# Where the eight S5 gate blocks stand, and VectorE's order, in a one-core backbone step

## The chip, the core and the metric

The kernel runs on one NeuronCore of a Trainium2 chip. The metric is the device time of one execution in microseconds (us). Five engines work side by side, each through its own queue in order: TensorE (PE in the rows, PEld its weight loads), VectorE (DVE), ScalarE (ACT), GpSimd (POOL) and SyncE (SP), which here only issues DMAs.

## The reference, cut to what matters

One step of a two-layer hybrid backbone over 1024 latent and 256 context tokens, in float32. The part around the change is the even layer: one projection of the modulated input, a bidirectional S5 state-space scan, and the gate with which the S5 output is multiplied.

```python
proj = h @ pe['w_in']
u_a, z_a, q, k, v, z_b = jnp.split(proj, [...], axis=-1)
y_a, hf_re, hf_im = _s5_bidir(u_a, ...)          # scan over the tokens, both directions
g_a = jax.nn.gelu(y_a)
y_a = g_a * jax.nn.sigmoid(g_a @ pe['w_glu'] + pe['b_glu'])
y_a = y_a * jax.nn.silu(z_a)                     # z_a: eight blocks of 128 columns, the "gate blocks"
...
o = _diff_attn(q_r, k_all, v_all, lam)           # keys and values: cached context and new ones
```

## The kernel before

All activations are held transposed, 128 channels by 1280 tokens (`NT`; 1024 latent and 256 context). A projection block of 128 columns is `project_steps`: three chunks of 512, 512 and 256 tokens, each eight steps over the 1024 input channels, each step three matmuls (`mm3`, lines 46 to 48: the float32 operands are split into a high and a low part). The function yields after half of each 512 chunk and after each chunk, so a block has five pieces. ScalarE and VectorE make the low part of the weights ahead (`split`, lines 41 and 42): starting block j emits the loads and the splits of block j + 1, and there are two sets of weight buffers.

A gate block is `z_steps`: after each chunk ScalarE takes a tanh out of PSUM (L907) and VectorE multiplies (L908), which frees the PSUM buffer (tag `acc`, four of them); at the end the 128 x 1280 result is written to `dZa` for a later stage.

`stage_a` ends with these parts. First the q and k blocks (`qk_block`), spread over two scans (`ssm.scan`, L527 to L583). A scan is a chain of small operations on VectorE, 31 steps of five (L527, L529, L530, L531, L532), then a correction loop (L579 to L583) in four parts, each written to memory (`dz`, L584). Outside of `manual_schedule` a planner sets each engine's order from costs of its own, not the source.

Then the S5 outputs, for j = 0 to 7, in pools of their own, which take over memory of the scan. `c_weights(j)` makes four groups of weights on VectorE (three operations each, L456 to L458), 24 small matmuls (`kp`, L612 to L614), copies to `kt` on ScalarE (L616), an addition to `kt` on VectorE (L620) and eight DMAs from `kt` to `m` (L623). `load_c(j)` loads `u` and `zc`. `c_out(j)` is 24 matmuls (`y`, L645 to L647), four GELUs on ScalarE (L649) and eight DMAs to `dG` that ScalarE's queue issues (L653). In iteration j, `c_weights(j + 1)` comes first, then gate block j + 1, then `c_out(j)`. Only TensorE is held to the order of the source there; the planner orders VectorE and ScalarE.

After the output of j = 4 stands `cache_parts`: four times, a 512 KB piece of the cached keys (twice) or values (twice) is loaded to a tile `cx`, split by ScalarE (`chi`, L41) and VectorE (`cx`, L42), and both parts are written back to memory, in four DMAs for keys and two for values. Its tiles come from the pool `zx`, which has three buffers and also holds the gate blocks' results. Attention (first matmuls L994) follows.

Of the kernel before, what the change touches and what calls it, by code (L numbers as in the profile page):

```python
# [10 lines left out]
F32 = mybir.dt.float32  # L11
# [10 lines left out]
NT = LS + LP  # L22
# [16 lines left out]
def split(nc, src, hi, lo, le=None):  # L39

    nc.scalar.copy(hi, src)  # L41
    (le or nc.gpsimd).tensor_sub(lo, src, hi.bitcast(F32))  # L42


def mm3(nc, out, whi, wlo, xhi, xlo, start, stop):
    nc.tensor.matmul(out, whi, xhi, start=start, stop=False)  # L46
    nc.tensor.matmul(out, whi, xlo, start=False, stop=False)  # L47
    nc.tensor.matmul(out, wlo, xhi, start=False, stop=stop)  # L48
# [318 lines left out]
class Weights:  # L367
# [5 lines left out]
    def next(s, key, steps=False):  # L373

        if s.gen is None:
            s.start()
        while s.step():
            pass
        w, s.gen = s.ahead, None
        assert s.rest.pop(0)[0] == key  # L380
        if s.rest and s.rest[0][1] is not None:
            s.start()
            while not steps and s.step():
                pass
        return w
# [16 lines left out]
def project(*args, **k):  # L402
    for _ in project_steps(*args, **k):
        pass
# [23 lines left out]
def raw_dma(nc, dst, src):  # L428

    nc.sync.dma_start(dst.bitcast(F32), src.bitcast(F32))  # L430
# [249 lines left out]
def stage_a(c, wp):  # L680

    nc, tc, a, o = c.nc, c.tc, c.a, c.o
    c.wlo = nc.vector
    dt = lambda n, shape, t=F32: [c.dram.tile(shape, t, name=f"{n}{i}") for i in range(HB)]
    c.dU = dt("dU", [128, 8, NCH])
    c.dG = dt("dG", [128, T, NCH])
    c.dQh, c.dQl = dt("dQh", [128, NT], F32R), dt("dQl", [128, NT], F32R)
    c.dK = [dt(f"dK{m}_", [128, NT], F32R) for m in range(2)]
    c.dZa = dt("dZa", [128, NT])
    with ExitStack() as es:  # L690
        pool = lambda n, b, **k: es.enter_context(tc.tile_pool(name=n, bufs=b, **k))
        ev = pool("ev", 2)
        ssm = Ssm(c)
        c.wfp = [c.wf1, pool("wf", 1)]

        def chunk(j, evac, i, w, part=(0, KC)):
            o, n = CH[i]
            if part[0] == 0:
                chunk.p = ps.tile([128, 512], F32, name="acc", tag="acc")
            for k in range(*part):  # L700
                mm3(nc, chunk.p[:, :n], w[0][:, k], w[1][:, k], c.hhi[:, k, o:o + n], c.hlo[:, k, o:o + n], k == 0, k == KC - 1)
            if part[1] == KC:
                evac(chunk.p[:, :n], o, n)

        def new_u(j):
            x = ev.tile([128, T, NCH], F32, name="x", tag="x")
            xv = x.rearrange("q t (k i) -> q t k i", i=NS)

            def evac(p, off, n):
                if off < LS:  # L710
                    nc.scalar.copy(xv[:, off // 128:off // 128 + 4, :, 1:], p.rearrange("q (t i k) -> q t k i", t=4, k=SEG))
                else:
                    nc.scalar.copy(xv[:, :, :, 0], p.rearrange("q (t c) -> q t c", c=CP))

            def done():
                for t in range(T):
                    nc.sync.dma_start(c.dU[j][t * N:(t + 1) * N].rearrange("n g c -> g n c"), x[:, t])
            return evac, done

        def u_block(j):  # L720
            evac, done = new_u(j)
            project(c, ps, c.w.next(('in', j)), c.hhi, c.hlo, evac)
            done()

        def qk_block(h, is_k):
            x = ev.tile([128, NT], F32, name="x", tag="x")
            sc = 1.0 if is_k else 0.125
            project(c, ps, c.w.next(('in', (24 if is_k else 16) + h)), c.hhi, c.hlo,
                    lambda p, off, n: nc.scalar.activation(x[:, off:off + n], p, AF.Copy, scale=sc))
            xs = rp.tile([128, LS], F32, name="xs")  # L730
            for q in range(4):
                nc.scalar.dma_start(xs[q * 32:(q + 1) * 32], x[(q ^ 1) * 32:(q ^ 1) * 32 + 32, 0:LS])
            if is_k:
                nc.scalar.dma_start(o['new_cache_k'][h], x[:, LS:NT])
            nc.vector.tensor_mul(x[:, 0:LS], x[:, 0:LS], rc[:, 0])
            nc.vector.tensor_mul(xs, xs, rc[:, 1])
            nc.vector.tensor_add(x[:, 0:LS], x[:, 0:LS], xs)
            hi = rp.tile([128, NT], F32R, name="xhi")
            lo = x.bitcast(F32R)
            split(nc, x, hi, lo, nc.vector)  # L740
            if is_k:
                for m in range(2):
                    for r, t in enumerate((hi, lo)):
                        raw_dma(nc, c.dK[m][h][r * 64:(r + 1) * 64], t[m * 64:(m + 1) * 64])
            else:
                raw_dma(nc, c.dQh[h], hi)
                raw_dma(nc, c.dQl[h], lo)

        ET = mybir.EngineType
        with tc.tile_pool(name="ps0", bufs=3, space=PSUM) as ps, tc.manual_schedule(engines={ET.PE, ET.DVE, ET.Activation, ET.Pool}):  # L750
            startup(c, ps, new_u, chunk)
        ps = pool("ps", 4, space=PSUM)
        c.sc = pool("ssk", 1, side="right")
        neg_lambda(c)
        ssm_tables(c)
        st = pool("sst", 2)
        ts = [ssm.c_tables(st, j) for j in range(2)]
        with tc.tile_pool(name="rp", bufs=1) as rp, tc.tile_pool(name="zp", bufs=1) as zp, \
                tc.tile_pool(name="ssb", bufs=2) as sb:
            for j in range(2, 4):  # L760
                u_block(j)
            z = ssm.new_z(zp, 0)
            ssm.powers(zp, 0)
            for j in range(4):
                ssm.b_side(sb, ps, j, z)
            rc = rp.tile([128, 2, LS], F32, name="rope")
            nc.sync.dma_start(rc, a['rope'])
            for j in range(4, 8):
                u_block(j)
            qk = [(h, is_k) for is_k in (True, False) for h in range(8)]  # L770

            def scan(h):
                for _ in ssm.scan(zp, h, z):
                    if qk:
                        qk_block(*qk.pop(0))

            for _ in range(KA):
                qk_block(*qk.pop(0))
            scan(0)
            z = ssm.new_z(zp, 1)  # L780
            ssm.powers(zp, 1)
            for j in range(4, 8):
                ssm.b_side(sb, ps, j, z)
            for _ in range(KB):
                qk_block(*qk.pop(0))
            scan(1)
            while qk:
                qk_block(*qk.pop(0))
        with tc.tile_pool(name="ssc", bufs=2) as sb, tc.tile_pool(name="zx", bufs=3) as zx:
            with tc.manual_schedule(engines={ET.PE}):  # L790
                def gate(j):
                    x = zx.tile([128, NT], F32, name="zx", tag="zx")
                    for _ in z_steps(c, ps, x, j):
                        pass
                    nc.sync.dma_start(c.dZa[j], x)

                gate(0)
                w = ssm.c_weights(sb, ps, 0, *ts.pop(0))
                uz = ssm.load_c(sb, 0)
                for j in range(8):  # L800
                    if j < 7:
                        nuz = ssm.load_c(sb, j + 1)
                        if j < 6:
                            ts.append(ssm.c_tables(st, j + 2))
                        nw = ssm.c_weights(sb, ps, j + 1, *ts.pop(0))
                        gate(j + 1)
                    ssm.c_out(sb, ps, j, *w, *uz)
                    w, uz = nw, nuz
                    if j == 4:
                        cache_parts(c, zx)  # L810
        c.wfp = [c.wf1]
    c.wlo = nc.gpsimd


KA, KB = 4, 2


def startup(c, ps, u_block, chunk):
# [82 lines left out]
def z_steps(c, ps, x, j, steps=False, late=None):  # L901

    nc = c.nc

    def evac(p, off, n):
        t = x[:, off:off + n]
        nc.scalar.activation(t, p, AF.Tanh, scale=0.5)  # L907
        nc.vector.scalar_tensor_tensor(t, t, 1.0, p, op0=OP.add, op1=OP.mult)  # L908
    return project_steps(c, ps, c.w.next(('in', 8 + j), steps), c.hhi, c.hlo, evac, late=late)
# [1119 lines left out]
```

## Time and profile before

| what | value |
|---|---|
| median of 3 runs | 2831.46 us (2827.33 to 2838.45) |
| the profiled execution | 2831.44 us, its span 2829.4 us |
| TensorE busy in the span | 2566.0 us (91%) |
| VectorE busy | 1772.5 us (63%) |
| ScalarE busy | 1075.5 us (38%) |
| mean granted TensorE clock | 0.958 of full speed |

All times in the rows are counted from the start of the span. Two stretches matter: the tail of the second scan (510 to 592 us) and the S5 outputs (592 to 807 us). In the rows, a letter q behind an engine's name (SPq, ACTq) marks its queue issuing a DMA, and the brackets hold the idle time before an instruction and what ended it.

### The profile page before, as it was taken

How to read it: one execution, taken by the hardware profiler on the slowest of the kernel's cores; microseconds unless marked ns; L12 is line 12 of the kernel's file. 1: busy time of each engine (PE TensorE's matmuls, PEld its weight loads, DVE VectorE, ACT ScalarE, POOL GpSimd, SP SyncE). 2: the span in 40 equal slices, each digit the busy share in tenths (PEclk: the TensorE clock that was granted, in tenths of full speed). 3: DMA queues.
4: the chain of work that ended last, by engine and by line, in shares of the span. 5: the costliest groups of instructions: out<-in, count | busy, mean ns of one | idle time of the engine just before them, and what ended most of it. 6: DMA issues, size and time to landing. Idle time of an engine off the chain costs nothing.

```text
span 2829.4 us, 40030 instructions
## 1 busy us (share of the span) xinstructions
PE 2566.0 (91%) x14905; PEld 2244.0 (79%) x14905; DVE 1772.5 (63%) x3636; ACT 1075.5 (38%) x2136; POOL 512.7 (18%) x434
## 2 busy tenths in 40 slices
PE   8999889159879999999988989988999999999998
PEld 6788778148768788887876878867999989999786
DVE  6879988984336787777876866675234435654332
ACT  3342243012246666666754221464223333322311
POOL 0000000000012332323331000005223334332321
PEclk9999999579999999999999999999999999999999
DMA  6445663256752222222226883322322136654422
GB/s 229 172 129 132 175 208 117 91 160 192 227 142 76 80 73 66 90 83 79 78 65 161 295 274 123 116 82 84 106 79 75 58 102 226 199 171 151 149 79 93
DMA packets 249130, 374.01 MB, mean 132 GB/s; under 512 B 39492, under 2 KB 172134, under 8 KB 245350
## 3 DMA queue, kind: packets, MB, share of 16 engines
q1 hardware_dynamic: 226376, 324.47, 36.7%
q10 hardware_dynamic: 22416, 46.33, 5.0%
q8 instruction: 117, 1.92, 0.3%
q14 instruction: 77, 0.63, 0.1%
q0 software_dynamic: 144, 0.66, 0.1%
HBM read 254.06 MB, written 104.73 MB: 127 GB/s over the span
## 4 chain that ended last, share of the span: by engine, by line
PE 46%; DVE 10%; ACT 5%; DMA 4%; issue 2%; POOL 2%; SPq 0%; DVEq 0%; ACTq 0%; POOLq 0%
PE pf L46 6%; PE pf L47 6%; PE pf L48 6%; PE oa L48 4%; PE oa L46 4%; PE oa L47 4%; PE acc L46 2%; PE acc L48 2%; PE acc L47 2%; ACT e L1020 2%; DVE mx L1010 2%; DVE atl L1054 2%; DMA owf<-w_out_o 1%; DVE e L1038 1%; PE atp L1050 1%
## 5 line engine op out<-in xcount | busy, mean ns | idle before, releaser
L46 PE MATMUL acc<-hhi,whi 128*128 128x512 f32 (+1 forms) x1152 | 421.2, 366 | 20.1 <-DVE zx L908 7.5
L48 PE MATMUL acc<-hhi,wlo 128*128 128x512 f32 (+1 forms) x1152 | 415.4, 362 | 25.8 <-DVE wlo L42 25.6
L47 PE MATMUL acc<-hlo,whi 128*128 128x512 f32 (+1 forms) x1152 | 417.1, 362 | 0.9 <-DVE hlo L218 0.2
L1041 POOL TENSOR_TENSOR e<-e,e 128x1024 f32<-128x1024 f32 x64 | 152.6, 2384 | 1124.6 <-ACT e L1040 850.9
L48 PEld LDWEIGHTS acc<-hhi,wlo 128*128 128x128 f32 x1152 | 221.6, 192 | 62.5 <-DVE wlo L42 31.3
L46 PEld LDWEIGHTS acc<-hhi,whi 128*128 128x128 f32 x1152 | 221.7, 192 | 58.5 <-ACT O L1063 11.1
L46 PE MATMUL oa<-owh,oyh 128*128 128x512 f32 x640 | 254.6, 398 | 8.2 <-DVE t L1379 5.1
L48 PE MATMUL oa<-owh,oyl 128*128 128x512 f32 x640 | 253.4, 397 | 1.0 <-POOL oyl L42 1.0
L47 PE MATMUL oa<-owl,oyh 128*128 128x512 f32 x640 | 254.1, 397 | 0.0
L47 PEld LDWEIGHTS acc<-hlo,whi 128*128 128x128 f32 x1152 | 221.6, 192 | 34.8 <-DVE hlo L218 4.6
L1020 ACT ACTIVATE e<-X,mx 128x1024 f32<-128x1024 f32 x128 | 142.9, 1116 | 121.2 <-DVE mx L1014 118.4
L41 ACT CAST whi<-wf 128x512 fp32r<-128x512 f32 x146 | 89.3, 620 | 208.7 <-DMA wf<-w_glu 41.8
L1010 DVE TENSOR_REDUCE mx<-X 128x1 f32<-128x1024 f32 x128 | 155.1, 1212 | 9.7 <-PE X L995 9.7
L42 POOL TENSOR_TENSOR wlo<-wf,whi 128x512 fp32r<-128x512 f32 x64 | 82.8, 1294 | 419.6 <-ACT whi L41 403.8
L46 PEld LDWEIGHTS oa<-owh,oyh 128*128 128x128 f32 x640 | 121.4, 190 | 38.6 <-ACT gt L1280 4.0
L42 DVE TENSOR_TENSOR wlo<-fold,whi 128x512 fp32r<-128x512 f32 x94 | 84.7, 914 | 106.5 <-ACT whi L41 105.5
L48 PEld LDWEIGHTS oa<-owh,oyl 128*128 128x128 f32 x640 | 121.4, 190 | 29.7 <-POOL oyl L42 1.4
L47 PEld LDWEIGHTS oa<-owl,oyh 128*128 128x128 f32 x640 | 121.5, 190 | 27.9
L1053 ACT CAST ath<-atp 128x512 fp32r<-128x512 f32 (+1 forms) x208 | 99.4, 514 | 103.1 <-PE atp L1050 101.6
L46 PE MATMUL pf<-heh,whi 128*128 128x322 f32 x400 | 126.1, 319 | 9.9 <-ACT heh L1549 8.3
L1054 DVE TENSOR_TENSOR atl<-atp,ath 128x512 fp32r<-128x512 f32 (+1 forms) x208 | 115.2, 578 | 17.0 <-ACT ath L1053 17.0
L47 PE MATMUL pf<-hel,whi 128*128 128x322 f32 x400 | 125.6, 314 | 0.1
(448 smaller groups left out, 6665.7 us busy)
## 6 DMA issues: line engine op xcount, KB each, us to landing
wf<-w_in_e SPq DMA_DIRECT2D x96, 256.0 KB
raw<-w_fno SPq DMA_DIRECT2D x16, 1024.0 KB
mw<-w_mod SPq DMA_DIRECT2D x24, 512.0 KB
stg<-w_modT SPq DMA_DIRECT2D x24, 512.0 KB
u<-dU SPq DMA_DIRECT2D x16, 640.0 KB
dz<-z SPq DMA_DIRECT2D x8, 1280.0 KB
zc<-dz SPq DMA_DIRECT2D x16, 640.0 KB
qh<-dQh SPq DMA_DIRECT2D x160, 64.0 KB
```

The costliest lines, as they stand in the source:

```text
L41: nc.scalar.copy(hi, src)
L42: (le or nc.gpsimd).tensor_sub(lo, src, hi.bitcast(F32))
L46: nc.tensor.matmul(out, whi, xhi, start=start, stop=False)
L47: nc.tensor.matmul(out, whi, xlo, start=False, stop=False)
L48: nc.tensor.matmul(out, wlo, xhi, start=False, stop=stop)
L1010: v.tensor_reduce(t.mx[:, 0, m:m + 1], t.X[m], axis=AX.X, op=OP.max, negate=True)
L1020: nc.scalar.activation(t.e[m][:, :LS], t.X[m], AF.Exp, bias=b, accum_out=t.sums[:, 0, m:m + 1])
L1038: v.scalar_tensor_tensor(e[0][:, :nk], e[1][:, :nk], t.r, e[0][:, :nk], op0=OP.mult, op1=OP.add)
L1041: nc.gpsimd.tensor_add(e[0][:, nk:], e[0][:, nk:], e[1][:, nk:])
L1050: nc.tensor.transpose(p[:, i], t.e[0][:, (b + i) * 128:(b + i + 1) * 128], c.ident)
L1053: nc.scalar.copy(hi, p[:, :w])
L1054: return lambda: v.tensor_sub(t.al[:, b:b + w, o], p[:, :w], hi.bitcast(F32))
```

## The change

Gate blocks 0 to 3 are now written at the end of the scan's part of the source, outside of `manual_schedule`, with result tiles from pool `ev`. Gate blocks 4 to 7 are one generator. `fill(n)` runs its next n pieces (halves of a 512 chunk, or the 256 chunk): two pieces before the outputs' loop, then two ahead of each `c_out(j)` and one behind it. That makes 2 + 3 per iteration, so the 20 pieces are used up in iteration 5. Within that part VectorE too is now held to the order of the source, `cache_parts` included.

```diff
             while qk:
                 qk_block(*qk.pop(0))
+            for j in range(GE):
+                x = ev.tile([128, NT], F32, name="x", tag="x")
+                for _ in z_steps(c, ps, x, j):
+                    pass
+                nc.sync.dma_start(c.dZa[j], x)
         with tc.tile_pool(name="ssc", bufs=2) as sb, tc.tile_pool(name="zx", bufs=3) as zx:
-            with tc.manual_schedule(engines={ET.PE}):
-                def gate(j):
-                    x = zx.tile([128, NT], F32, name="zx", tag="zx")
-                    for _ in z_steps(c, ps, x, j):
-                        pass
-                    nc.sync.dma_start(c.dZa[j], x)
-
-                gate(0)
+            with tc.manual_schedule(engines={ET.PE, ET.DVE}):
+                def gates():
+                    for j in range(GE, 8):
+                        x = zx.tile([128, NT], F32, name="zx", tag="zx")
+                        yield from z_steps(c, ps, x, j)
+                        nc.sync.dma_start(c.dZa[j], x)
+                rest = gates()
+
+                def fill(n):
+                    for _ in range(n):
+                        next(rest, None)
+                fill(2)
                 w = ssm.c_weights(sb, ps, 0, *ts.pop(0))
                 uz = ssm.load_c(sb, 0)
                 for j in range(8):
...
                         nw = ssm.c_weights(sb, ps, j + 1, *ts.pop(0))
-                        gate(j + 1)
+                    fill(2)
                     ssm.c_out(sb, ps, j, *w, *uz)
+                    fill(1)
                     w, uz = nw, nuz
                     if j == 4:
                         cache_parts(c, zx)
+                fill(100)
...
+GE = 4
```

What this does to the engines' orders, at three places. All other rows of the five queues, from attention on, stand as before.

VectorE in the second scan, one piece of the difference (+ the changed kernel). L531 and L532 end a scan step, L920 is the changed kernel's number for the gate's multiplication, `wlo` the low part of a block's weights.

```order
 L531 TENSOR_TENSOR m_4096<-m_4096,z 128x320
+L920 SCALAR_TENSOR_TENSOR x<-x,acc 128x256
 L532 TENSOR_TENSOR z<-m_4096,m_4097 128x64x5
+L42 TENSOR_TENSOR wlo<-wf,whi 128x512
 L527 TENSOR_TENSOR m_4103<-A8r,z 128x320
 L529 TENSOR_TENSOR m_4104<-A8i,z 64x320
 L530 TENSOR_TENSOR m_4104<-A8i,z 64x320
 L531 TENSOR_TENSOR m_4103<-m_4103,z 128x320
+L42 TENSOR_TENSOR wlo<-wf,whi 128x512
 L532 TENSOR_TENSOR z<-m_4103,m_4104 128x64x5
+L920 SCALAR_TENSOR_TENSOR x<-x,acc 128x512
```

Sixteen such instructions come into the scan: ten multiplications (seven of 512 columns and three of 256: gate blocks 1 to 3 and the first chunk of block 4) and six splits of weights (for blocks 3, 4 and 5).

VectorE around the caches, before: one split of a cached piece stands among the weights of j = 6, three more behind the weights and the `kt` of j = 7.

```order
L457 TENSOR_TENSOR t_6415<-tab,tabc 128x576
L42 TENSOR_TENSOR cx<-cx,chi 128x1024
L458 TENSOR_TENSOR cw_6413<-t_6414,t_6415 128x576
...
L620 TENSOR_TENSOR kt<-kt,dd 16x8x16
L42 TENSOR_TENSOR cx<-cx,chi 128x1024 x3
L908 SCALAR_TENSOR_TENSOR zx<-zx,acc 128x512 x2
```

And after, the same place: all four stand in a row, right behind the multiplication of gate block 7's first chunk and ahead of the weights of j = 6.

```order
L920 SCALAR_TENSOR_TENSOR zx<-zx,acc 128x256
L42 TENSOR_TENSOR wlo<-wf,whi 128x512 x2
L920 SCALAR_TENSOR_TENSOR zx<-zx,acc 128x512
L42 TENSOR_TENSOR cx<-cx,chi 128x1024 x4
L456 TENSOR_TENSOR t_6336<-tab,tabc 128x576
L457 TENSOR_TENSOR t_6337<-tab,tabc 128x576
L458 TENSOR_TENSOR cw_6335<-t_6336,t_6337 128x576
```

SP's queue at that place, after: the loads of `cx` and the writes of its parts follow each other, behind the loads of `u` and `zc` of j = 6, with the DMAs to `m` of j = 6 behind them. Before, DMAs of the outputs (`m`, `zc`, `u`, `dZa`) stood between them.

```order
L445 DMA u<-dU_92 128x1280
L632 DMA zc<-dz_151 128x2x640
L351 DMA wf<-w_in_e 128x512
L665 DMA cx<-cache_k 128x4x256
L430 DMA dKc_6289<-chi 64x1024
L430 DMA dKc_6289<-cx 64x1024
L430 DMA dKc_6290<-chi 64x1024
L430 DMA dKc_6290<-cx 64x1024
L665 DMA cx<-cache_k 128x4x256
```

ScalarE's four `chi` casts likewise stand in a row now, behind the DMA issues to `dG` of j = 4 and the tanh of gate block 7's first chunk.

## Rows read from the trace of the kernel before

**Rows 1.** Waits of TensorE, 510 to 803 us: who waited, total us, times, longest.

```profile
PE kp L612 <- DVE cw L458: 82.3, 3, 81.4
```

**Rows 2.** Busy us of each engine in stretches (count), granted clock, DMA share, GB/s.

```profile
core 0: us, PE busy (x) PEld busy (x) DVE busy (x) ACT busy (x) POOL busy (x), PEclk, DMA share, GB/s
510.00:592.00 82.00, 0.57 (x5) 0.39 (x5) 74.00 (x167) 3.81 (x8) 0.00 (x0) 0.52 0.29 96
592.00:611.00 19.00, 11.89 (x96) 7.76 (x95) 18.48 (x28) 2.19 (x4) 0.00 (x0) 0.68 0.78 225
660.00:685.00 25.00, 25.00 (x172) 22.38 (x172) 12.36 (x21) 6.26 (x13) 0.00 (x0) 1.00 0.72 204
```

**Rows 3.** ScalarE in time, start us, us: tanh behind gate chunks 512, 512, 256.

```profile
714.42 0.60 ACT L907 ACTIVATE zx<-acc 128x512 f32<-128x512 f32 x1 [0.30 <-PE acc L48]
719.86 0.60 ACT L907 ACTIVATE zx<-acc 128x512 f32<-128x512 f32 x1 [4.84 <-PE acc L48]
722.73 0.38 ACT L907 ACTIVATE zx<-acc 128x256 f32<-128x256 f32 x1 [2.27 <-PE acc L48]
```

**Rows 4.** VectorE in time, in the second scan, with and without an inserted instruction.

```profile
519.80 0.48 DVE L532 TENSOR_TENSOR z<-m,m 128x320 f32<-128x320 f32 x1
520.20 0.68 DVE L42 TENSOR_TENSOR wlo<-wf,whi 128x512 fp32r<-128x512 f32 x1
520.80 0.48 DVE L527 TENSOR_TENSOR m<-A8r,z 128x320 f32<-128x320 f32 x1
...
522.86 0.49 DVE L532 TENSOR_TENSOR z<-m,m 128x320 f32<-128x320 f32 x1
523.39 0.49 DVE L527 TENSOR_TENSOR m<-A8r,z 128x320 f32<-128x320 f32 x1
```

**Rows 5.** The scan's end: the last write of `dz` (SP), and VectorE behind it.

```profile
584.86 0.51 SPq L584 DMA_DIRECT2D dz<-z  x1
...
590.80 0.28 DVE L618 TENSOR_TENSOR dd<-ident,Dn 16x128 f32<-16x128 f32 x1 [4.63 <-DMA dz<-z]
```

**Rows 6.** VectorE in time: ends of two following groups of output weights.

```profile
593.32 0.76 DVE L458 TENSOR_TENSOR cw<-t,t 128x576 f32<-128x576 f32 x1
...
595.58 0.76 DVE L458 TENSOR_TENSOR cw<-t,t 128x576 f32<-128x576 f32 x1
```

**Rows 7.** TensorE in time: two following groups of `kp` without a wait.

```profile
603.68 0.38 PE L612 MATMUL kp<-cw,tab 128*16 128x128 f32 x2
...
604.14 0.38 PE L612 MATMUL kp<-cw,tab 128*16 128x128 f32 x2
```

**Rows 8.** ScalarE in time: the last two GELUs of an output, the DMA issues behind.

```profile
703.30 0.44 ACT L649 ACTIVATE gt<-y 128x320 f32<-128x320 f32 x1 [1.19 <-PE y L647]
704.93 0.44 ACT L649 ACTIVATE gt<-y 128x320 f32<-128x320 f32 x1 [1.19 <-PE y L647]
705.40 5.66 ACTq L653 DMA_DIRECT2D dG<-gt  x8
```

**Rows 9.** The caches' fourth piece: its load (SP), its splits (ScalarE, VectorE).

```profile
760.85 0.57 SPq L667 DMA_DIRECT2D cx<-cache_v  x1
...
767.62 1.04 ACT L41 CAST chi<-cx 128x1024 fp32r<-128x1024 f32 x1 [9.44 <-DMA dG<-gt]
...
768.69 1.23 DVE L42 TENSOR_TENSOR cx<-cx,chi 128x1024 fp32r<-128x1024 f32 x1 [9.25 <-ACT chi L41]
```

**Rows 10.** The last output: a DMA ahead of its last six `m` (SP), then TensorE.

```profile
785.95 0.57 SPq L632 DMA_DIRECT2D zc<-dz  x1
...
795.81 0.87 PE L645 MATMUL y<-u,m 128*128 128x160 f32 x2 [6.63 <-DMA wf<-w_in_e]
...
803.90 0.43 PE L647 MATMUL y<-zc,cw 128*128 128x160 f32 x2
807.14 0.47 PE L994 MATMUL X<-kx,qh 128*128 128x512 f32 x1 [2.81 <-DMA dG<-gt]
```

**Rows 11.** Bandwidth while only the last `dz` write runs (columns as in Rows 2).

```profile
586.00:590.00 4.00, 0.00 (x0) 0.00 (x0) 0.17 (x1) 0.00 (x0) 0.00 (x0) 0.50 0.97 311
```

## The prediction

> **What bounds the kernel now.** I read the waits of TensorE first, then the busy time of the engines by stretches, then single engines in time. The largest wait of TensorE in this part of the program is a hole of 81.4 us in front of the first `kp` matmul, ended by VectorE [rows 1]. The stretch 510 to 592 us shows why: TensorE works 0.57 us, VectorE 74 of 82 us, on the serial second scan [rows 2]. [...] A block is two chunks of 5.4 us and one of 2.9 us [rows 3], 13.7 us.
>
> **The change, step by step, on the clock of the rows.**
>
> *What goes into the hole.* Blocks 1 to 3 and the first chunk of block 4 move there: 3 x 13.7 + 5.4 = 46.5 us of TensorE, from 510 to 557 us, so they fit. VectorE pays: 16 instructions come into its scan. With one of 512 columns, the next scan instruction starts 1.00 us after L532, without one 0.53 us [rows 4]. The inserted work also fills a dependency gap, so each costs 0.47 us, and 16 x 0.47 is 7.5 us (the three of 256 columns less, say 6.7 in all). I looked for new waits: the first multiplication stands after L531 at about 522.9 us, when the chunk computed from 510.2 has been out for 7 us, and TensorE stays ahead by 4 us or more at all ten. So the scan ends at 584.8 + 6.7 = 591.5 us.
>
> *A wait that is covered.* Before, VectorE then waited 4.63 us for the last `dz` write, 5.9 us after its issue [rows 5]. In the new order two whole groups of weights stand ahead of the first instruction that takes over that memory, 2.3 us each [rows 6], with 1.4 us of the third: 6.0 us, just the cover. I take this 4.6 us as won; it is lost again if the memory is taken over in another order.
>
> *Behind the scan VectorE's order is the source's.* Making the weights of one j takes 4 x 2.3 = 9.2 us [rows 6]. Then four last `kp` groups at 0.46 us [rows 7], 1.9 us, and copy and addition to `kt`, some 0.9 us. Before, VectorE made weights ahead of need. Now they start only when the multiplications that the source has ahead of them are done. j = 0 takes 9.2 + 2.8 us and j = 1 9.2 + 1.9, so TensorE reaches the pieces of iteration 0 at 614.6 us.
>
> An output is 4 x 1.63 = 6.5 us of TensorE [rows 8]. Where the piece behind an output ends a chunk (j = 0, 3, 4, 5), its tanh stands on ScalarE behind the last GELU (0.4 us) and eight DMA issues (5.7 us, rows 8), and the multiplication behind that: 6.9 us (256 columns) or 7.4 us after the output's end. Only then come the next weights, 11.1 us to their last `kp`.
> - j = 0: 614.6 + 5.4 + 6.5 + 6.9 + 11.1 = 644.5.
> - j = 1, no chunk ends behind the output, and the weights run beside TensorE: 5.4 + 6.5 + 2.7 + 3.7, to 662.8.
> - j = 2: pieces of 5.6 us, then on VectorE 2.3 us of multiplications and splits and 11.1 of weights, to 681.8; TensorE's own work ends as late.
> - j = 3: 5.4 + 6.5 + 7.4 + 11.1, to 712.2.
> - j = 4: 5.6 + 6.5, output done at 724.3.
>
> *The caches.* This is the large term. VectorE now meets the four `cx` splits in a row, ahead of the weights of j = 6, and nothing else is left to it or TensorE. The pieces can't overlap: of the three `zx` buffers gate block 7 holds one, `cx` and `chi` take two, so each load waits for the writes of the piece before. SP issues the first load when `u`, `zc` and `wf` are issued, 1.8 us after output 4. A load beside other traffic took 6.8 us to its cast, and the two splits end 2.3 us after the cast begins [rows 9]: 735.2. For a quiet load no row stands alone. The nearest is the `dz` write: 1.31 MB in 5.9 us [rows 5] at 311 GB/s [rows 11] is 4.2 us of transfer and 1.7 us of fixed time. By that 512 KB take 3.4 us, and with the rest of the writes beside them 3.7. The writes add about 3.5 us for keys and 2.4 for values. So two more pieces cost 3.5 + 3.7 + 2.3 = 9.5 each and the last 8.4, and VectorE is free at 762.6. The bounds: with 3.0 us loads and 2.5 us writes the chain is 6 us shorter, with 6.8 us loads and 4.5 us writes 13 us longer. I take the quiet price, since SP's other DMAs are queued behind the chain.
>
> *The end of the part.* Weights of j = 6, to 773.7; j = 5: 5.4 + 6.5 + 6.9 + 11.1, to 803.6; output 6 to 810.1. The last output waits for its `m`. [...] Attention's first matmul came at 807.1, 2.8 us after output 7 [rows 10]; its loads now are issued early enough, so it follows at about 825.7.
>
> **Sum.** 825.7 - 807.1 = 18.6 us later, and behind that nothing moves. The profiled execution took 2831.44 us, two hundredths below the median: 2831.4 + 18.6 = 2850 us. What was won (46.5 us of TensorE and 4.6 us of a wait, less 6.7 us) is spent on some 38 us at the caches and gaps of 7 to 9 us at the weights of j = 2, 5 and 7.
>
> [...]
>
> **Rivals.**
> 1. *The caches don't hold VectorE.* If the four pieces were through when VectorE arrives, the weights of j = 6 would start some 30 us earlier: 2820. The caches took from 715 to 770 us before, so this needs loads far ahead, and SP's order speaks against it.
> 2. *Interleaving pays in full.* If the gaps at the weights closed too, TensorE's work alone would count: 2831.4 - 46.5 + 6.7 - 4.6 = 2787. For it speaks the hole of 81 us; against it VectorE's order, in which weights stand behind multiplications of late chunks. [...]
> 3. *The chain is short and the issues quick.* 6 us less at the caches, 3 us for eight `dG` issues instead of 5.7 (three times): 2850 - 14 = 2836, no change.
> 4. *The chain is slow.* Loads as beside traffic: 2850 + 13 = 2863.
> 5. *The scan itself is held.* If weights of blocks 3 or 4 land late, a multiplication in VectorE's scan waits for its chunk, up to 5.4 us each, twice: 2850 + 9 = 2859. TensorE's lead of 4 us and more speaks against it.
>
> **Chances.** Forecast 0.52, rival 1 0.08, rival 2 0.07, rival 3 0.15, rival 4 0.12, rival 5 0.06. I take 0.5%, 14.2 us, as what a measurement of this kernel can tell from no change, so above 2845.6 is slower. A quarter of the forecast's chance (own range 2838 to 2860) lies below that: 0.13. Same is 0.13 + 0.08 + 0.15 = 0.36 and slower 0.39 + 0.12 + 0.06 = 0.57. The range leaves out rival 2 and most of rival 1 below, and a chain slower than rival 4's above: 2824 to 2866.
>
> **What would show it.** Right, if VectorE's scan ends near 591.5 us without waits at L920; if TensorE idles 35 to 45 us in front of a `kp` late in the stage, with VectorE waiting at `cx`; and if gaps of 7 to 9 us stand before three other `kp`. Wrong, if the `cx` splits are through in under 15 us (rival 1), if the `kp` gaps are absent (rival 2), or if L920 waits in the scan (rival 5).

## The result, and the profile after

| what | before | after |
|---|---|---|
| median | 2829.39 us (2826.95 to 2838.45, 4 runs) | 2859.68 us (2857.26 to 2869.76, 4 runs) |
| ratio to before, 95% interval | | 1.0108 (1.0074 to 1.0142) |
| the profiled execution, its span | 2831.44 us, 2829.4 us | 2857.54 us, 2855.5 us |
| first `kp` matmul | 591.90 us | 590.01 us |
| attention's first matmul | 807.14 us | 833.02 us |

The median of before is that of its runs beside the changed kernel. The kernel became slower by 30 us (26 us between the two profiled executions). The range held, and so did the sign; the likeliest time, 2850, was 10 us too low. Of the 26.1 us by which the span grew, 25.9 were there when attention began.

TensorE in time, in the changed kernel: start us, us, what, and in brackets the idle time ahead and what ended it. First the hole that [rows 1] showed, then the waits among the outputs, then attention.

```profile
590.01 0.58 PE L612 MATMUL kp<-cw,tab 128*16 128x128 f32 x2 [41.22 <-DVE cw L458]
...
631.96 0.59 PE L612 MATMUL kp<-cw,tab 128*16 128x128 f32 x2 [6.69 <-DVE cw L458]
...
699.68 0.58 PE L612 MATMUL kp<-cw,tab 128*16 128x128 f32 x2 [6.75 <-DVE cw L458]
...
766.83 0.59 PE L612 MATMUL kp<-cw,tab 128*16 128x128 f32 x2 [43.40 <-DVE cw L458]
...
800.22 0.58 PE L612 MATMUL kp<-cw,tab 128*16 128x128 f32 x2 [8.18 <-DVE cw L458]
...
824.68 0.87 PE L645 MATMUL y<-u,m 128*128 128x160 f32 x2 [7.12 <-DMA m<-kt]
...
833.02 0.50 PE L1006 MATMUL X<-kx,qh 128*128 128x512 f32 x1
```

The hole of 81.4 us is half filled: 41.2 us remain. Sum up the rest: 6.7 + 6.8 + 43.4 + 8.2 + 7.1 = 72 us of new waits, where the kernel before had 17: 6.6 and 2.8 us in [rows 10], and this one.

```profile
770.57 0.80 PE L46 MATMUL acc<-hhi,whi 128*128 128x512 f32 x1 [7.54 <-DVE zx L908]
```

The new waits stand ahead of the `kp` of j = 2, 5, 6 and 7 and of the last output.

VectorE behind the multiplication of gate block 7's first chunk: the four `cx` splits, and the first weight of j = 6.

```profile
730.01 0.69 DVE L920 SCALAR_TENSOR_TENSOR zx<-zx,acc 128x512 f32<-128x512 f32 x1 [16.11 <-ACT zx L919]
734.08 1.23 DVE L42 TENSOR_TENSOR cx<-cx,chi 128x1024 fp32r<-128x1024 f32 x1 [3.38 <-ACT chi L41]
744.57 1.23 DVE L42 TENSOR_TENSOR cx<-cx,chi 128x1024 fp32r<-128x1024 f32 x1 [9.26 <-ACT chi L41]
755.36 1.23 DVE L42 TENSOR_TENSOR cx<-cx,chi 128x1024 fp32r<-128x1024 f32 x1 [9.57 <-ACT chi L41]
763.33 1.23 DVE L42 TENSOR_TENSOR cx<-cx,chi 128x1024 fp32r<-128x1024 f32 x1 [6.74 <-ACT chi L41]
764.47 0.75 DVE L456 TENSOR_TENSOR t<-tab,tabc 128x576 f32<-128x576 f32 x1
```

Each split waits for its cast, each cast for its load, and each load for the writes of the piece before. On SP (queue issues) the second load follows the last write of the first piece by 3 us:

```profile
727.66 0.40 SPq L665 DMA_DIRECT2D cx<-cache_k  x1
...
736.51 0.61 SPq L430 DMA_DIRECT2D dKc<-cx  x1
739.52 0.38 SPq L665 DMA_DIRECT2D cx<-cache_k  x1
...
749.91 0.37 SPq L667 DMA_DIRECT2D cx<-cache_v  x1
...
758.18 0.38 SPq L667 DMA_DIRECT2D cx<-cache_v  x1
```

The small gaps have another origin. ScalarE at the end of output 4: the last GELU, eight DMA issues, and behind them the tanh for which VectorE's row at 730.01 waited 16 us.

```profile
720.73 0.44 ACT L649 ACTIVATE gt<-y 128x320 f32<-128x320 f32 x1 [1.19 <-PE y L647]
721.20 8.14 ACTq L653 DMA_DIRECT2D dG<-gt  x8
729.38 0.60 ACT L919 ACTIVATE zx<-acc 128x512 f32<-128x512 f32 x1 [8.22 <-DMA dG<-gt]
```

Behind the gaps of 43.4 and 8.2 us TensorE worked at a granted clock of 0.50 of full speed (the column behind the engines, in the two stretches of `kp`). Two following `kp` groups in the second stand behind it:

```profile
766.00:777.00 11.00, 7.69 (x49) 5.12 (x50) 7.43 (x11) 1.94 (x4) 0.00 (x0) 0.50 0.06 26
797.00:811.00 14.00, 8.07 (x51) 5.51 (x52) 9.37 (x15) 2.58 (x5) 0.00 (x0) 0.50 0.47 146
```

```profile
803.71 0.63 PE L612 MATMUL kp<-cw,tab 128*16 128x128 f32 x2
...
804.57 0.63 PE L612 MATMUL kp<-cw,tab 128*16 128x128 f32 x2
```

A group took 0.86 us there, against 0.46 in [rows 7].

### The profile page after: what moved, and what is told of

It is laid out like the page before. It is cut to its first block, busy times and chain, and to the rows that moved or that the text cites. A ratio compares the mean times of both kernels' runs of the same rounds, so it can differ in the third digit from the quotient of the medians.

```text
span 2855.5 us, 40017 instructions
## 1 busy us (share of the span) xinstructions
PE 2572.4 (90%) x14905; PEld 2246.7 (79%) x14905; DVE 1771.3 (62%) x3636; ACT 1076.8 (38%) x2136; POOL 512.2 (18%) x434
## 4 chain that ended last, share of the span: by engine, by line
PE 45%; DVE 11%; ACT 5%; DMA 3%; issue 2%; POOL 1%; SPq 0%; DVEq 0%; ACTq 0%; POOLq 0%
PE pf L47 6%; PE pf L46 6%; PE pf L48 6%; PE oa L48 4%; PE oa L46 4%; PE oa L47 4%; ACT e L1032 2%; DVE mx L1022 2%; PE acc L46 2%; PE acc L48 2%; PE acc L47 2%; DVE atl L1066 2%; DVE e L1050 1%; DMA owf<-w_out_o 1%; ACT e L1033 1%
## 5 line engine op out<-in xcount | busy, mean ns | idle before, releaser
L46 PE MATMUL acc<-hhi,whi 128*128 128x512 f32 (+1 forms) x1152 | 419.6, 364 | 11.7 <-ACT O L1075 6.5
L47 PEld LDWEIGHTS acc<-hlo,whi 128*128 128x128 f32 x1152 | 220.6, 192 | 34.2 <-DVE hlo L218 4.6
L612 PE MATMUL kp<-cw,tab 128*16 128x128 f32 x128 | 32.6, 348 | 109.4 <-DVE cw L458 109.4
L1062 PE MATMUL atp<-ident,e 128*128 128x128 f32 x672 | 107.1, 287 | 21.9 <-DVE atl L1066 14.6
```

The source lines that it names most:

```text
L612: nc.tensor.matmul(kp[:, i, 112:240], bb[0], cw[0][:, g, 0:128], start=True, stop=False)
L1062: nc.tensor.transpose(p[:, i], t.e[0][:, (b + i) * 128:(b + i + 1) * 128], c.ident)
```

## The experiments

Ratios are to the kernel before, run beside each on the same chip (its medians: 2830.66 us beside e1 to e4, 2832.19 beside e5 to e8, 2832.23 beside e9 to e11, 2833.24 beside e12); "to before" is the difference of the medians in us. The text below compares the medians of two rows as they stand; as the medians of before lie between 2829.4 and 2833.2, such a difference can be off by up to 4 us where the two rows are not from one of these groups.

| run | edit | us | to before | ratio, 95% interval |
|---|---|---|---|---|
| the change | | 2859.68 | +30.3 | 1.0108 (1.0074 to 1.0142) |
| e1 | change, `cx` splits on GpSimd | 2841.47 | +10.8 | 1.0043 (1.0029 to 1.0057) |
| e2 | change, VectorE planned | 2810.52 | -20.1 | 0.9926 (0.9911 to 0.9941) |
| e3 | before, VectorE in source order | 2865.68 | +35.0 | 1.0122 (1.0107 to 1.0137) |
| e4 | before, four blocks moved | 2815.78 | -14.9 | 0.9955 (0.9941 to 0.9968) |
| e5 | change, caches in the scan | 2833.20 | +1.0 | 1.0005 (0.9995 to 1.0014) |
| e6 | e5, VectorE planned | 2788.61 | -43.6 | 0.9846 (0.9832 to 0.9861) |
| e7 | e6, six blocks moved | 2796.04 | -36.2 | 0.9879 (0.9862 to 0.9895) |
| e8 | change, `dG` issued by GpSimd | 2851.17 | +19.0 | 1.0072 (1.0055 to 1.0089) |
| e9 | e5, no piece behind an output | 2793.99 | -38.2 | 0.9867 (0.9852 to 0.9882) |
| e10 | before, caches in the scan | 2819.91 | -12.3 | 0.9963 (0.9949 to 0.9977) |
| e11 | e7, `dG` issued by GpSimd | 2788.06 | -44.2 | 0.9844 (0.9829 to 0.9859) |
| e12 | e11, five blocks moved | 2798.41 | -34.8 | 0.9884 (0.9868 to 0.9901) |

### The change taken apart: the order, and the moved blocks (e2, e3, e4)

e2 has the change's places with only TensorE held; e3 has the places of before with VectorE held; e4 moves blocks 0 to 3 and leaves blocks 4 to 7 whole, VectorE planned.

```diff
 e2, to the changed kernel:
-            with tc.manual_schedule(engines={ET.PE, ET.DVE}):
+            with tc.manual_schedule(engines={ET.PE}):
 e3, to the kernel before:
-            with tc.manual_schedule(engines={ET.PE}):
+            with tc.manual_schedule(engines={ET.PE, ET.DVE}):
 e4, to the kernel before:
+            for j in range(GE):
+                x = ev.tile([128, NT], F32, name="x", tag="x")
+                for _ in z_steps(c, ps, x, j):
+                    pass
+                nc.sync.dma_start(c.dZa[j], x)
...
-                gate(0)
...
-                        gate(j + 1)
+                        if j + 1 >= GE:
+                            gate(j + 1)
```

> The changed kernel with only TensorE held to the source's order; the gate blocks stand where the change puts them. Theory, what the change loses is lost by VectorE's order: without it the kp gaps of 6 to 8 us and the 43 us gap go, and the blocks moved into the hole pay: about 2800 (2790 to 2812). Rival, the pieces spread over the outputs are themselves the loss (each tanh behind eight DMA issues on ScalarE): the gaps stay, with another engine named, and the time is 2825 or more.

> The kernel before with VectorE also held to the source's order, no gate block moved. Theory, the order alone costs: each group of weights then waits for the gate block ahead of it, 11 us of weights behind a 6.5 us output, 4 to 5 us at six outputs (27 us), and the caches hold VectorE some 25 us more: about 2880 (2865 to 2895). Rival, the order costs little where whole blocks of 13.7 us stand between: within 10 us of the kernel before.

> The kernel before with gate blocks 0 to 3 moved into the second scan and nothing else: blocks 4 to 7 stay whole at their places, VectorE stays planned. Theory, the moved blocks pay by themselves nearly in full, 55 us of TensorE less the 7 to 9 us that VectorE's scan grows: about 2790 (2780 to 2805). Rival, with four blocks fewer the outputs are bound by loads, weights or the caches' chain, which took from 715 to 770 us before: half the gain or less, 2810 or more.

Measured: 2810.5, 2865.7 and 2815.8 us. The moved blocks gain 15 us (e4), with the other four spread 20 us (e2), and VectorE's order loses 35 us (e3, against before) to 50 us (the change, against e2). So the loss is the order's. All three missed their middle: e2 and e4 gained 11 and 26 us less than expected (e4's rival came true), and e3 lost 14 us less. TensorE's waits say why. e4's theory counted one block too many: block 0 already stood in the hole before (its tanh instructions run at 501 to 511 us), so three blocks, 41 us, could move and not four. And two outputs that did not wait before now wait 8.8 and 6.8 us for ScalarE's copies to `kt`, which stand behind `dG` issues (the profiled execution of e4 was 8 us above its median):

```profile
641.79 0.90 PE L645 MATMUL y<-u,m 128*128 128x160 f32 x2 [8.78 <-ACT kt L616]
```

In e2 (planned) two outputs wait, and behind 610 us no other wait of TensorE is 2 us or longer:

```profile
754.83 0.90 PE L645 MATMUL y<-u,m 128*128 128x160 f32 x2 [21.38 <-ACT kt L616]
777.03 0.87 PE L645 MATMUL y<-u,m 128*128 128x160 f32 x2 [13.87 <-DMA m<-kt]
```

There the caches' chain holds too, by another way: ScalarE's copies to `kt` and SP's DMAs to `m` stand behind casts of cached pieces and behind their loads and writes. And in e3 (in order, whole blocks) the expected 4 to 5 us at each of six outputs are absent. Between 605 and 820 us one wait of TensorE is over 2 us long:

```profile
766.32 0.59 PE L612 MATMUL kp<-cw,tab 128*16 128x128 f32 x2 [35.79 <-issue]
```

That is the caches again (VectorE waits 34.2 us there at its four `cx`). So in e3 the long waits that the order brings are at the caches; the small gaps belong to the pieces' place. e2 also has the wait that I had called covered, back in the planned order, with the length that it has in [rows 5] (the profile names no releaser for it here):

```profile
596.31 0.28 DVE L618 TENSOR_TENSOR dd<-ident,Dn 16x128 f32<-16x128 f32 x1 [4.69 <-issue]
```

### The caches' chain (e1, e5, e6, e10)

```diff
 e1, in cache_parts of the changed kernel:
-            split(nc, x, hi, lo, nc.vector)
+            split(nc, x, hi, lo, nc.gpsimd)
```

> The changed kernel with one word changed: GpSimd instead of VectorE makes the low parts of the cached keys and values, so VectorE's order has no cx in it. My theory is that the four cx splits in VectorE's queue are the large loss: VectorE would begin the weights of j = 6 at about 731 instead of 764.5, the gap in front of that kp falls from 43.4 to about 10 us, and the time falls by 30 us or so, to about 2826. Rival A, the chain of loads and writes holds the outputs anyway because the DMAs to m stand behind it on SP: the gap moves to a y or a later kp and the time stays above 2848. Rival B, the splits on GpSimd are so slow that the chain ends later than the outputs and attention waits for its keys: TensorE's first X then waits for kx, and the gain is under 15 us.

Measured 2841.5: 18 us off the change and not 30. The gap ahead of j = 6 did fall, from 43.4 to 10.4 us, but ahead of j = 7 it grew from 8.2 to 16.8. ScalarE, then VectorE, show where the chain went: the tanh of gate block 7's last chunk stands behind the cast of the fourth piece, which waits 9.3 us for its load.

```profile
775.91 1.04 ACT L41 CAST chi<-cx 128x1024 fp32r<-128x1024 f32 x1 [9.32 <-DMA cx<-cache_v]
...
776.86 0.38 ACT L919 ACTIVATE zx<-acc 128x256 f32<-128x256 f32 x1
```

```profile
777.27 0.42 DVE L920 SCALAR_TENSOR_TENSOR zx<-zx,acc 128x256 f32<-128x256 f32 x1 [20.46 <-ACT zx L919]
```

So rival A came true in part, on ScalarE's queue and not on SP's. A smaller part of the miss is GpSimd's own: beside two of its splits a VectorE instruction among these weights took longer, 3.8 us in all (last section). To take the chain away, and not one engine's share in it, e5 and e6 move it into the scan, into buffers that the q and k blocks leave there; e10 does that to the kernel before.

```diff
 e5, to the changed kernel:
+            cache_parts(c, rp)
             for j in range(GE):
...
-                    if j == 4:
-                        cache_parts(c, zx)
...
-            x = sb.tile([128, NT], F32, name="cx", tag="zx")[:, :LS]...
+            x = sb.tile([128, LS], F32, name="cx", tag="xs")...
...
-            hi = sb.tile([128, NT], F32R, name="chi", tag="zx")...
+            hi = sb.tile([128, NT], F32R, name="chi", tag="xhi")...
 e6: e5 with manual_schedule(engines={ET.PE})
 e10: the same edit in the kernel before
```

> The changed kernel with the four cached pieces loaded, split and written during the second scan, in the two buffers that the q and k blocks leave; VectorE stays in the source's order. With GpSimd in VectorE's place the chain only moved to ScalarE, whose casts held the tanh of the last gate chunks. Theory, the chain as such costs what the gap shows: kp of j = 6 follows the multiplication at 730 us and not the splits at 764, 31.5 us, less four splits of 1.14 us in the scan, 27 us in all: about 2833 (2826 to 2840). Rival, something else is late in its place (loads of zc or u, m, the scan held by a split that waits for its load): 2845 or more.

> The same, with only TensorE held to the source's order. With VectorE planned and the caches in their old place, TensorE still waited 21.4 and 13.9 us in front of two outputs, behind casts of cached pieces and behind DMAs to m that stood after them on SP. Theory, these two waits are the chain as well: 35 us less 4.6 us in the scan, less some late m that stays (7 us): about 2787 (2778 to 2796). Rival, TensorE is held by the outputs' own loads there: 2800 or more.

> The kernel before with nothing changed but the caches' place: in the second scan, no gate block moved, VectorE planned. It tells how much of the gain of the run with planned VectorE and caches in the scan (2789) is the caches' alone. Theory, the chain cost the kernel before its waits of 7.5 us at 770 and 6.6 us at 795 us at most, less 4.6 us in the scan: about 2821 (2814 to 2829), so the four moved gate blocks are worth the other 30 us and more. Rival, the chain cost nothing in the kernel before: 2832 to 2838.

Measured 2833.2, 2788.6 and 2819.9, each within 2 us of the theory. The chain cost the change 26 us (2859.7 to 2833.2; 29 by the column "to before"), e2 22 us and the kernel before 12 us. With the caches in the scan in both, the change's places with VectorE planned are worth 31 us (e10 to e6). In e5 the `kp` of j = 6 is one small gap among four:

```profile
645.12 0.59 PE L612 MATMUL kp<-cw,tab 128*16 128x128 f32 x2 [6.38 <-DVE cw L458]
...
713.53 0.59 PE L612 MATMUL kp<-cw,tab 128*16 128x128 f32 x2 [7.40 <-DVE cw L458]
...
747.49 0.58 PE L612 MATMUL kp<-cw,tab 128*16 128x128 f32 x2 [10.21 <-DVE cw L458]
...
779.19 0.58 PE L612 MATMUL kp<-cw,tab 128*16 128x128 f32 x2 [8.14 <-DVE cw L458]
```

### The small gaps (e8, e9)

```diff
 e8, in c_out of the changed kernel:
-            nc.scalar.dma_start(dst[t], gt[t * N:(t + 1) * N])
+            nc.gpsimd.dma_start(dst[t], gt[t * N:(t + 1) * N])
 e9, to e5:
-                    fill(2)
+                    fill(3)
                     ssm.c_out(sb, ps, j, *w, *uz)
-                    fill(1)
```

> The changed kernel with the eight DMAs to dG of each output issued by GpSimd's queue and not by ScalarE's. Theory, the tanh of a chunk that ends behind an output waits for these issues, and the weights wait for its multiplication: the kp gaps of 6.7, 6.75 and 8.2 us (j = 2, 5, 7) shrink to under 2 us each, the 43 us gap stays within 2 us (its loads only come earlier with all the rest), and attention's first exponent no longer waits for issues: about 2840 (2834 to 2847). Rival, the gaps are set by the chunk's own matmuls and by the weights, 4.6 us to the first kp, and stay within 2 us: 2853 or more. [...]

> The run with the caches in the scan and VectorE in the source's order, with one more edit: three pieces stand ahead of each output and none behind it. TensorE there still waited 6.4, 7.4, 10.2 and 8.1 us in front of the kp of j = 2, 5, 6 and 7, just those ahead of which a chunk ends behind an output. Theory, only this place costs: with the chunk's end ahead of the 6.5 us output, the 4.6 us of weights to the first kp run beside the output and these four gaps shrink to 2 us or less: about 2808 (2800 to 2817). Rival, holding VectorE to the source's order costs wherever the pieces stand (weights never ahead of need): gaps of 4 us and more at most of the kp, and 2825 or more.

e8 took 2851.2, 8.5 us under the change where 20 were expected, and above the expected range. The gaps ahead of j = 2, 5 and 7 about halved but did not go, so the DMA issues are about half their cause; the rest is the multiplication and the weights behind it. The gap ahead of j = 6, expected to stay, fell from 43.4 to 38.3 us. And one new gap came (684.54):

```profile
633.68 0.58 PE L612 MATMUL kp<-cw,tab 128*16 128x128 f32 x2 [3.55 <-DVE cw L458]
...
684.54 0.59 PE L612 MATMUL kp<-cw,tab 128*16 128x128 f32 x2 [8.59 <-DVE cw L458]
...
711.62 0.58 PE L612 MATMUL kp<-cw,tab 128*16 128x128 f32 x2 [3.66 <-issue]
...
800.44 0.58 PE L612 MATMUL kp<-cw,tab 128*16 128x128 f32 x2 [3.22 <-DVE cw L458]
```

Its cause is VectorE's order once more: a split of weights for a later gate block stands ahead of the weights of j = 4, and waits for a load that SP issued late, at 673.1 us (in the changed kernel at 655.1).

```profile
679.89 0.69 DVE L42 TENSOR_TENSOR wlo<-wf,whi 128x512 fp32r<-128x512 f32 x1 [12.36 <-ACT whi L41]
```

e9 is the sharper test. With the third piece ahead of the output, all four gaps are gone: no wait of TensorE for VectorE is longer than 1.9 us between 615 and 764 us, and one wait remains:

```profile
764.04 0.87 PE L645 MATMUL y<-u,m 128*128 128x160 f32 x2 [10.19 <-DMA dG<-gt]
```

The time fell by 39 us to 2794.0, more than expected (2808) and below the expected range, in part as I had left 7 us of gaps in place. Between the profiled executions, from the first `kp` to attention, it is 33 us (208.0 to 174.9), about the four gaps of e5 (32.1 us). Of the other 6 us, 3.3 lie ahead of the first `kp`, where the source is the same, and 2.8 behind attention's first matmul; their cause stays open. VectorE held to the source's order is then 5.4 us from VectorE planned (e6, with the pieces at their old places). So nearly all of the cost was not the holding, but what the order put ahead of the weights.

### How much of the hole can be used (e7, e11, e12)

```diff
 e7, to e6:
-GE = 4
+GE = 6
 e11: e7, with the dG DMAs on nc.gpsimd
 e12: e11, with GE = 5
```

> Six gate blocks and the cached pieces in the second scan, two blocks left in half chunks among the outputs, only TensorE in the source's order. Theory, what is left of the hole (46 us with four blocks) takes two more blocks of 13.7 us for 10 more VectorE instructions at 0.47 us: 22 us under the run with four blocks, about 2765 (2755 to 2780). Rival, with so little gate work left the outputs are bound by the weights (9.2 us each) and loads, and the two blocks bring nothing: 2785 or more.

> The run with six gate blocks and the caches in the scan, VectorE planned, with the DMAs to dG issued by GpSimd. There the outputs came 20.7 us apart, each waiting 5 to 8.5 us for kt or m, and ScalarE's copies to kt stood behind 10.9 us of issues to dG. Theory, those issues bind it: without them the five waits of TensorE (36 us) shrink by half or more and the time falls by 18 to 30 us, to about 2772. Rival, the transfers bind it (77% of the DMA engines' time is taken there): 2788 or more.

> Five gate blocks and the cached pieces in the second scan, three blocks in half chunks among the outputs, VectorE planned, the DMAs to dG issued by GpSimd: between the run with four blocks (2789), where TensorE had no gap from 613 to 749 us, and that with six (2788 with GpSimd's issues), where it waited 5 to 6 us before several kp and y. Theory, the fifth block takes 13.7 us out of a stretch that TensorE still sets, for 2.3 us in the scan, and the gaps only come with the sixth: about 2778 (2769 to 2785). Rival, the gaps come with the fifth block already: 2786 to 2792.

Measured 2796.0, 2788.1 and 2798.4: the rivals of e7 and e11 were right (e11's at its edge), and e12 came out above its theory and its rival. Two more blocks in the hole gain nothing, since the outputs then wait for their own chain. In e7 five outputs wait, 36 us in all, as this one; ScalarE's copies to `kt` stand behind 10.8 us of issues:

```profile
738.21 10.84 ACTq L653 DMA_DIRECT2D dG<-gt  x8
749.17 1.90 ACT L616 COPY kt<-kp 16x480 f32<-16x480 f32 x4 [10.98 <-DMA dG<-gt]
```

```profile
749.77 0.90 PE L645 MATMUL y<-u,m 128*128 128x160 f32 x2 [8.27 <-DMA dG<-gt]
```

Issuing from GpSimd gave back 8 us of those 36 (e11), not half. e11's rival blamed the transfers, with 77% of the DMA engines' time taken (700 to 760 us in e7); but e6 has 84% at 700 to 745 us, and TensorE has no wait of 1.5 us there. What e11 shows in the place of the issues is the next queue: ahead of two of its `kp` (gaps of 4.9 and 5.9 us) VectorE waits 8.0 and 9.0 us for tables (`tab`, `tabc`), which SP issued behind pairs of `zc` loads that held it for 11.7 and 9.5 us. The second of them:

```profile
701.31 0.76 DVE L456 TENSOR_TENSOR t<-tab,tabc 128x576 f32<-128x576 f32 x1 [9.01 <-DMA tabc<-ssm_c]
```

```profile
703.70 0.59 PE L612 MATMUL kp<-cw,tab 128*16 128x128 f32 x2 [5.89 <-DVE cw L458]
```

Five blocks (e12) were 10 us slower than six with the same issues. VectorE's waits for tables are there too (7.8, 9.2 and 6.5 us, against 8.0, 9.0 and 4.7 in e11), so they hardly tell the two apart. TensorE's waits of 1.5 us and more behind 640 us add up to nearly the same, 24.9 us against 26.5, so the fifth block's 13.7 us came on top of them; why it did not run inside them stays open. The fastest versions are e6 and e11, at 0.985 of before.

## Why the prediction was right, and where it was off

All its times are on the clock of the rows of before. The changed kernel's profiled execution ran 3 to 5 us ahead of that clock when the scan began, by chance: e1 and e8, which have the same code up to the outputs, reached their first `kp` at 593.98 and 593.12 us, the changed kernel at 590.01. So the measured times below are 3 to 5 us earlier than they would be on the forecast's clock.

| step | forecast | measured |
|---|---|---|
| the scan grows by | 6.7 us | 8.1 us |
| wait for the last `dz` | gone | gone |
| last `kp` of j = 2 | 644.5 | about 640.4 |
| output 4 done | 724.3 | 720.7 |
| VectorE through the caches | 762.6 | 764.5 |
| last `kp` of j = 6 | 773.7 | 776.6 |
| last `kp` of j = 7 | 803.6 | 810.2 |
| output 7 done | 825.3 | 833.3 |
| attention's first matmul | 825.7 | 833.0 |

- **The hole and the scan** were right. That a block moved there frees time of TensorE among the outputs, [rows 2] show at 660 to 685 us; in the changed kernel too it was busy for all of 640 to 690 us, at a granted clock of 1.00, and VectorE for 23.5 us of them. From the first L527 of the second scan to the issue of its last `dz` VectorE took 159.2 us (428.58 to 587.76), against 151.1 (433.78 to 584.86) before. Its one wait at L920 there was 1.1 us, so rival 5 was wrong.
- **The covered wait** was right: VectorE goes from the scan into the weights without it, and e2, with the planned order, has a wait of 4.69 us at that place again.
- **The gaps** were right in place and size: forecast 7 to 9 us ahead of j = 2, 5 and 7, measured 6.7, 6.8 and 8.2; at j = 3 and 4 none, as forecast. e9 shows the mechanism. The eight `dG` issues of [rows 8] (5.7 us) took 5.9 and 5.3 us ahead of the first two gaps and 7.3 us ahead of the third; in five of the eight outputs it was 7.3 to 8.5 us from the first issue to the end of the last.
- **The caches** were right as the largest term and too small by 5.5 us: from output 4 to VectorE's release 43.8 us (720.7 to 764.5) against 38.3. The first load was issued 7.0 us after the output and not 1.8: the `zc` ahead of it on SP waited 3.6 us, and the load itself 2.2 us more. It then took 5.3 us to its cast, not 6.8; the row behind the 6.8 [rows 9] names a `dG` DMA and not the load as what ended that wait, so it was no clean price of a load, and here it offset part of the miss by luck. Two intervals were 10.5 and 10.8 us, not 9.5; the last was 8.0, not 8.4. The writes, estimated at 3.5 us for keys and 2.4 for values, took 4.2, 4.1 and 1.6 us from a split's end to the next load's issue. Rival 4 had the sign of this miss and more than twice its size. The prediction's short bound does not follow from its own terms: 3.0 us loads and 2.5 us writes make the three intervals 4.0 us shorter (7.8 with the first load), not 6.
- **The clock** is a term that the sum leaves out. Behind the gaps of 43.4 and 8.2 us it stood at 0.50 (766 to 777 and 797 to 811 us), and a `kp` group took 0.86 us where I used 0.46. (Output 7 began at 0.50 too, at 824.6 to 828 us, as it did before at 795.8 to 799 us; it took 8.6 us, against 8.5 in [rows 10].) From the caches to the last `kp` of j = 7 that and the longer issues (1.6 us) made 4.7 us: 6.6 us late there against 1.9.
- **The last output** started 7.1 us after TensorE had finished output 6 (forecast 6.7), as the `zc` among its `m` held SP. The forecast has that `zc` at 806.9, the start 9.9 us later at 816.8, and 8.5 us for the output, both lengths from [rows 10]: 825.3, and attention at 825.7. No run shows these sums; measured were 824.7 for the start, 833.3 for the end and 833.0 for attention's first matmul. Attention followed output 7 at once. Its first matmul came 25.9 us later than before and the span's end 26.1: behind it nothing moved, as forecast.

Together: the sum's 18.6 us, 5.5 more at the caches, some 5 of slow restarts and issues and 1.4 in the scan give 30 us, which is what the medians differ by. That the profiled execution shows 26 fits its early start.

Rival 1 (the caches don't hold VectorE) was wrong for this kernel, but e5, which makes it true, came out at 2833. Rival 2 (interleaving pays in full, 2787) was wrong for this kernel too; e6 and e9 reach 2789 and 2794 with the same four blocks moved, but with the caches in the scan as well, which alone gained 12 us (e10). Interleaving did not pay in the change (2859.7 us) and did in e9 (2794.0), where the piece that stood ahead of the weights is covered by an output.

## What to carry to other kernels

When an engine is switched from a planner's order to the source's, list what the source puts ahead of its critical instructions: here a chunk's multiplication, behind eight DMA issues on another engine, and four splits that wait for loads, stood ahead of weights that needed neither. Put such pieces ahead of work that covers them, or into a stretch where the engine waits anyway: one piece moved across an output was worth 39 us here, the caches' chain 26. To test whether a chain binds, take away the chain and not one engine's share in it, as it moves to the next queue (e1).

## What the runs showed of the hardware

In e1 the split on GpSimd took 2.34 us (once 2.40), and two VectorE instructions on weights that began within one took 2.90 and 2.38 us, not the 0.75 or 0.76 that they take elsewhere. The first pair:

```profile
737.66 2.34 POOL L42 TENSOR_TENSOR cx<-cx,chi 128x1024 fp32r<-128x1024 f32 x1 [736.34 <-ACT chi L41]
```

```profile
737.71 2.90 DVE L457 TENSOR_TENSOR t<-tab,tabc 128x576 f32<-128x576 f32 x1
```

And the second:

```profile
777.03 2.34 POOL L42 TENSOR_TENSOR cx<-cx,chi 128x1024 fp32r<-128x1024 f32 x1 [8.02 <-ACT chi L41]
```

```profile
777.61 2.38 DVE L456 TENSOR_TENSOR t<-tab,tabc 128x576 f32<-128x576 f32 x1
```

The extra time, 2.15 and 1.62 us, is close to what GpSimd's instruction still had to run, 2.29 and 1.76 us; GpSimd's had begun 0.05 and 0.58 us ahead. A third VectorE instruction that began within a split, the gate's multiplication at 777.27, took 0.42 us, as it does without a split beside it (715.63). What held the two, no run shows.

Eight DMA issues to `dG` mostly took 4.2 us on GpSimd in e8 (about 0.53 us each) and 5.3 to 8.5 us on ScalarE in the changed kernel, up to 10.8 us in e7.
